# How many column pairs have their first two products made before the second tokens are normalised: nine and nine in place of five and six

## The chip, the cores and the metric

The kernel is one layer of a diffusion backbone on one core of a Trainium2 chip. A core has TensorE (PE) for matrix products, with weight loads (PEld) beside the products, VectorE (DVE), ScalarE (ACT), GpSimd (POOL) and SyncE (SP), from which this kernel issues its transfers between DRAM and the on-chip memory. Each engine works through its own list of instructions in order and waits on semaphores for the others. Products land in PSUM, from where ACT or DVE fetch them.

The metric is the device time of one execution in microseconds (us), as a median of several runs.

## The reference

1024 latent tokens and 256 context tokens of width 1024 in float32. Each layer is a half step of a gated feed-forward network, then the mixers (a short convolution and attention, merged by gates), then a second half step. Ahead of each stands a normalisation with shift and scale:

```python
x = x + 0.5 * ml[2] * swiglu(modulate(rms_norm(x, norm1_g), ml[0], ml[1]), ffn1_w_in, ffn1_w_out)
hx = modulate(rms_norm(x, norm2_g), ml[3], ml[4])
bg_l, cg_l, vc_l, q_l, k_l, v_l, gt_l = jnp.split(hx @ w_in, SPLITS, axis=-1)
...
x = x + ml[5] * merge_branches(y_conv_l, o_l, gt_l, w_branch_conv, w_branch_attn, w_out)
x = x + 0.5 * ml[8] * swiglu(modulate(rms_norm(x, norm3_g), ml[6], ml[7]), ffn2_w_in, ffn2_w_out)
return rms_norm(x, final_g)
```

What matters here are two of its products: `hx @ w_in` in the mixers, of which 20 pairs of blocks of 128 columns are made in the way described below (queries, keys and values go another way), and the product with `ffn2_w_in` in the second half step, 22 pairs.

## The kernel before

**Three products for one.** Each float32 operand is split into a high part (a copy rounded to float32r, by ACT) and a low part (the difference, by DVE), function `split`. A product is then three matmuls: high by high, high by low, low by high.

**Pairs of columns, seven products.** The latent tokens stand transposed on the chip, in two halves: the first 512 tokens (`C0`) and the second 512 (`C1`). Class `Winograd` makes a pair of column blocks for both halves at once, by Strassen's scheme in Winograd's form: the inner dimension of 1024 is cut in two, the weights of the pair form a 2 by 2 block matrix and the tokens another, and seven block products replace eight. Each product (`product(i)`) has four inner steps of three matmuls 128 x 128 by 128 x 512, twelve in all. Its left operand is a block of weights or a sum of blocks (POOL makes the sums `s1`, `s2`, `s3` and one more; `parts` splits each), its right operand is `self.r[i]`, four split tiles made from the normalised tokens. `r[1]` and `r[2]` need the first tokens alone. `r[3]` to `r[7]` need the second tokens too.

The order within a pair is fixed: `first` makes products 1 and 2 and keeps `u` (product 1) and `c` (their sum). `second` makes 6, 7 and 4, `third` makes 5 and 3, and each adds its products to the running sums on DVE.

**Started pairs.** `norm1` normalises the second tokens: sums of squares over the partitions and a broadcast on PE, and then, for each of four steps `k`, two scalings on DVE, two shifts on ACT, four differences on DVE, and five tiles of `r` that are split (ACT and DVE). While this goes on PE has only products 1 and 2 to make. So `start` makes them for the first `n_ahead` pairs, with the steps of `norm1` in between:

```python
for i in range(self.n_ahead):
    t = wpool.tile([P, 2, 512], F32, tag="wh", name=uniq("uc"), bufs=W_BUFS)
    u, c = t[:, 0], t[:, 1]
    act.copy(out=u, in_=self.product(1))
    run(norm, 1)
    dve.tensor_add(out=c, in0=u, in1=self.product(2))
    if i < RESIDENT:
        self.started.append((u, c))
    else:
        self.put_aside(t)
run(norm)
```

`norm1` has six steps (the sums, the broadcast, and the four `k`). `uc` takes two of the four `wh` buffers for good until its pair is finished (`RESIDENT` is 2); the other started pairs share the remaining two, and `put_aside` stores each to DRAM (`ucd`, 512 KB, from SP). When a pair's turn comes, `next_first` takes it out of `started`, and `fetch` brings `u` and `c` of the pair behind it back, one pair ahead, into two of the 11 buffers `t` (two loads of 256 KB). A pair that wasn't started goes through `first` in its turn.

**Weights.** The generator `lefts` gives the split left operands in the order in which they are used. For the first `n_ahead` pairs it loads the first block alone (a `raw` buffer of 512 KB, three of them) and splits its two halves; in the turn of a pair it loads both blocks (2 x 512 KB), lets POOL form the sums, and skips the two halves that have been used. Four `wl` buffers hold split operands, so ACT and DVE work up to four products ahead.

**Order.** The program is written in one order, and a planner in the compiler of the kernel places the instructions on the engines by its own costs: of what is ready, what was written earlier goes first; buffers of a pool are given out in the same way. What the planner put down is fixed in the program, and each engine follows it.

**Where it stands.** In the mixers `mix` (line 1027) takes its number from `AH2`; `mix.start(norm1)` (line 1071) begins when the first half step's output product is done, and its turns follow in the loop at 1088, with the context tokens' normalisation `normc2` (two steps after a pair) and the convolution's DVE instructions in between. In the second half step `fast` (line 1461) takes its number from `AH3`; its `start` is called in `ffn` (line 759) behind the output projection of the mixers, and its turns follow, two pairs at a time with their part of the output product. The first half step has a start of its own (`start_together`, `AH1`).

Of the kernel before, what the change touches and what calls it, by code (L numbers as in the profile page):

```python
# [41 lines left out]
STEPS = (0, 6, 6, 6, 7, 7, 8, 8, 8, 15)  # L42
WAIT = 4
AH1, WH = 8, (4, 5, 6, 7, 10, 11, 14, 15)
RESIDENT, AH2, AH3 = 2, 5, 6
SLOT = 1024


# [1526 lines left out]
```

## Time and profile before

| | us |
|---|---|
| median of 3 runs | 2805.99 (2802.83 to 2806.69) |
| the profiled execution | 2801.0 |
| its span, from the first instruction to the last | 2799.2 |
| PE busy | 2716.4 |
| DVE busy | 1956.4 |
| ACT busy | 1105.1 |
| POOL busy | 502.6 |

The mean granted clock of TensorE was 0.987 of full speed. The profile's instruction groups bear the line of a helper (88) throughout, so they are told apart by their tiles: `ps<-r,wl` are the matmuls of `Winograd`, `wl<-raw` and `wl<-s` the splits of weights and of sums of weights, `r<-nt` and `r<-h` the splits of right operands, `uc<-uc,ps` the sum that ends a started pair. Matmuls overlap, so the busy time of one is longer than the time until the next begins. A time in square brackets is how long an engine stood idle before an instruction, with the instruction whose end it waited for.

### The profile page before, as it was taken

The page shows a single profiled execution, that of the slowest core. Times are in us where ns is not written, and L with a number is a line of the kernel's source. Part 1 is how long each engine was busy: PE and PEld are TensorE (multiplying, and loading weights), DVE is VectorE, ACT ScalarE, POOL GpSimd, SP SyncE. Part 2 cuts the span into 40 slices and gives each one's busy share as a digit, 9 for nine tenths or more (in the row PEclk, how much of TensorE's full clock was granted, in tenths as well). Part 3 has the DMA queues.
Part 4 walks back from the last instruction along what each step waited for, and adds up shares of the span by engine and source line. Part 5 has one row for each costly group of instructions (what it writes and reads, how often), then busy time and mean ns, then how long its engine had stood idle before and what let it go on. Part 6 is the DMA issues. An engine that isn't in the chain of part 4 may idle for free.

```text
span 2799.2 us, 36980 instructions
## 1 busy us (share of the span) xinstructions
PE 2716.4 (97%) x13741; PEld 2280.3 (81%) x13741; DVE 1956.4 (70%) x3269; ACT 1105.1 (39%) x2177; POOL 502.6 (18%) x383
## 2 busy tenths in 40 slices
PE   7898999999999989999999999999998999999998
PEld 4687988888888867888999888877886788888887
DVE  5887688877854398676478676675458766666667
ACT  4524333333433243333244665674235222332225
POOL 2240122121000043323023111000002221212110
PEclk8899999999999999999999999999999999999999
DMA  8264434445974333322312321002433311111111
GB/s 305 95 204 156 143 107 128 131 145 162 314 237 126 103 123 106 98 90 77 119 33 84 95 80 46 27 31 80 158 91 103 101 46 46 61 61 53 46 53 68
DMA packets 355229, 302.96 MB, mean 108 GB/s; under 512 B 25558, under 2 KB 284776, under 8 KB 355048
## 3 DMA queue, kind: packets, MB, share of 16 engines
q1 hardware_dynamic: 355048, 300.59, 33.3%
q8 instruction: 108, 1.77, 0.3%
q14 instruction: 73, 0.60, 0.1%
HBM read 251.73 MB, written 48.76 MB: 107 GB/s over the span
## 4 chain that ended last, share of the span: by engine, by line
PE 54%; DVE 4%; ACT 1%; issue 1%; DMA 1%; DVEq 0%; ACTq 0%
PE ps L88 48%; PE po L88 3%; PE pt L88 3%; DVE wl L88 1%; DVE xb L88 0%; DMA raw<-in_ffn_w_out_dram 0%; DVE r L88 0%; DVE u L88 0%; DVE nt L88 0%; DVE ol L88 0%; DVE wo L88 0%; ACT pts L88 0%; DVE pts L88 0%; ACT pl L88 0%; DVE uc L88 0%
## 5 line engine op out<-in xcount | busy, mean ns | idle before, releaser
L88 PE MATMUL ps<-r,wl 128*128 128x512 f32 x5280 | 1237.7, 393 | 31.8 <-ACT wl L88 9.6
L88 PEld LDWEIGHTS ps<-r,wl 128*128 128x128 f32 x5280 | 992.2, 189 | 250.2 <-ACT wl L88 11.9
L88 POOL TENSOR_TENSOR s<-raw 128x512 f32<-128x512 f32 x64 | 100.7, 1573 | 1100.0 <-DVE r L88 377.5
L88 ACT CAST wl<-s 128x512 fp32r<-128x512 f32 x256 | 158.3, 620 | 318.9 <-PE ps L88 266.3
L88 ACT CAST wl<-raw 128x512 fp32r<-128x512 f32 x230 | 142.5, 621 | 251.9 <-PE ps L88 170.6
L88 DVE TENSOR_TENSOR wl<-raw,wl 128x512 fp32r<-128x512 f32 x228 | 163.0, 715 | 96.9 <-ACT wl L88 95.9
L88 POOL TENSOR_TENSOR s<-raw,s 128x512 f32<-128x512 f32 x64 | 102.5, 1601 | 686.1 <-DVE wl L88 682.5
L88 DVE TENSOR_TENSOR wl<-s,wl 128x512 fp32r<-128x512 f32 x256 | 215.8, 844 | 9.7 <-ACT wl L88 7.7
L88 PE MATMUL ps<-hid,wh 128*128 128x512 f32 x704 | 217.2, 390 | 0.7 <-ACT wh L88 0.7
L88 DVE SCALAR_TENSOR_TENSOR x<-ps,gate_l,x 128x512 f32<-128x512 f32 (+1 forms) x200 | 140.7, 726 | 76.7 <-PE ps L88 76.5
L88 ACT CAST wh<-raw 128x1024 fp32r<-128x1024 f32 (+2 forms) x92 | 89.4, 976 | 198.0 <-PE ps L88 167.8
L88 PEld LDWEIGHTS ps<-hid,wh 128*128 128x128 f32 x704 | 131.7, 188 | 29.5 <-ACT wh L88 1.6
L88 DVE SCALAR_TENSOR_TENSOR macc<-rawm,silu_c,macc 128x512 f32<-128x512 f32 x168 | 140.8, 856 | 15.2 <-DMA rawm<-in_w_mod_dram 14.1
L88 PE MATMUL ps<-hid,wo 128*128 128x512 f32 (+1 forms) x552 | 147.8, 381 | 2.3 <-DVE x L88 2.3
L88 DVE TENSOR_TENSOR u<-u,ps 128x512 f32<-128x512 f32 x168 | 114.2, 680 | 45.4 <-PE ps L88 45.0
L88 DVE TENSOR_TENSOR wl<-raw,wh 128x1024 fp32r<-128x1024 f32 (+1 forms) x84 | 98.4, 1172 | 65.5 <-ACT wh L88 64.0
L88 PE MATMUL ps<-wh,r 128*128 128x256 f32 x768 | 141.6, 285 | 0.0
L88 DVE TENSOR_TENSOR pts<-pt,pts 128x512 fp32r<-128x512 f32 x160 | 108.6, 686 | 43.1 <-ACT pts L88 41.9
L88 PE MATMUL ps<-hid,wl 128*128 128x512 f32 x352 | 136.5, 389 | 0.0
L88 PE MATMUL ps<-gh,wo 128*128 128x512 f32 (+1 forms) x368 | 135.0, 380 | 0.0
L88 DVE TENSOR_REDUCE m<-ps 128x1 f32<-128x512 f32 (+1 forms) x192 | 110.9, 595 | 26.6 <-PE ps L88 25.6
L88 ACT CAST pts<-pt 128x512 fp32r<-128x512 f32 x160 | 93.1, 593 | 86.2 <-PE pt L88 84.6
(254 smaller groups left out, 4784.4 us busy)
## 6 DMA issues: line engine op xcount, KB each, us to landing
raw<-in_ffn_w_in_dram SPq DMA_DIRECT2D x114, 512.0 KB, 3.7
raw<-in_ffn_w_out_dram SPq DMA_DIRECT2D x76, 512.0 KB, 4.3
rawm<-in_w_mod_dram SPq DMA_DIRECT2D x128, 256.0 KB, 3.9
raw<-in_w_in_dram SPq DMA_DIRECT2D x57, 512.0 KB, 3.6
hid<-hd SPq DMA_DIRECT2D x44, 256.0 KB, 6.1
rawm<-in_w_mod_dram SPq DMA_DIRECT2D x16, 512.0 KB, 7.3
xd<-x SPq DMA_DIRECT2D x32, 256.0 KB, 2.5
x<-xd SPq DMA_DIRECT2D x32, 256.0 KB, 5.9
```

The source lines that it names most:

```text
L88: inst = getattr(self.engine, name)(*args, **kw)
```

## The change

One line of constants. `RESIDENT` stays at 2.

```diff
-RESIDENT, AH2, AH3 = 2, 5, 6
+RESIDENT, AH2, AH3 = 2, 9, 9
```

Nine pairs of the 20 in the mixers, and nine of the 22 in the second half step, have their first two products made in `start`; seven of each nine are stored to DRAM and fetched in their turn, where it were three and four. The six steps of `norm1` are written between the first six of them in both places; in the mixers the sixth stood behind the fifth pair. The pairs 6 and up (counted from 0) are written behind all of `norm1`, and with the last of them the loads and POOL sums for the first pair's turn. The products, and what is computed, stay the same.

## The prediction

> **What bounds the kernel now.** I read the page first: busy times, then the 40 slices, then the stages by windows.
>
> ```profile
> PE 2716.4 (97%) x13741; PEld 2280.3 (81%) x13741; DVE 1956.4 (70%) x3269; ACT 1105.1 (39%) x2177; POOL 502.6 (18%) x383
> PEclk8899999999999999999999999999999999999999
> PE 54%; DVE 4%; ACT 1%; issue 1%; DMA 1%; DVEq 0%; ACTq 0%
> ```
>
> TensorE sets the time: 97% busy, and the chain that ended last is mostly PE. The change adds and removes no matmul, so all it can win is time in which PE stood still or ran at a low clock, in the two stages that it touches. The windows view, in slices of 10 us (busy us and instruction count of PE, PEld, DVE, ACT, POOL, then granted clock, DMA share, GB/s), shows them. The first row is the yardstick.
>
> ```profile
> 1100.00:1200.00 100.00, 100.00 (x443) 82.82 (x442) 68.47 (x106) 32.09 (x55) 30.52 (x22) 1.00 0.29 90
> 990.00:1000.00 10.00, 6.16 (x21) 4.62 (x20) 10.00 (x18) 6.78 (x12) 0.73 (x1) 0.84 0.26 105
> 1000.00:1010.00 10.00, 7.54 (x27) 4.54 (x26) 9.32 (x16) 5.26 (x10) 8.49 (x2) 0.98 0.64 210
> 1010.00:1020.00 10.00, 8.16 (x25) 6.04 (x25) 8.45 (x10) 5.75 (x13) 3.30 (x2) 0.66 0.01 2
> 1020.00:1030.00 10.00, 9.07 (x40) 6.98 (x39) 9.13 (x18) 2.62 (x5) 3.34 (x2) 1.00 0.47 144
> 2130.00:2140.00 10.00, 5.03 (x23) 3.83 (x21) 10.00 (x15) 5.22 (x9) 4.54 (x3) 1.00 0.44 158
> 2140.00:2150.00 10.00, 9.25 (x27) 6.58 (x28) 9.96 (x14) 4.26 (x8) 3.70 (x3) 0.66 0.36 106
> 2150.00:2160.00 10.00, 7.71 (x30) 5.08 (x29) 9.15 (x11) 4.98 (x9) 4.31 (x3) 1.00 0.15 52
> 2160.00:2170.00 10.00, 8.87 (x39) 6.78 (x38) 8.56 (x13) 3.66 (x6) 2.44 (x2) 1.00 0.32 99
> ```
>
> 443 matmuls in 100 us are one per 0.2257 us, or 44.3 in a slice. I count matmuls, not busy time, because a matmul at half clock counts as busy twice as long. Mixers (the stage that starts near 963): 21 + 27 + 25 + 40 = 113 where 177.2 fit, so 64.2 are missing, **14.5 us**. Second half step (it starts near 2100): 23 + 27 + 30 + 39 = 119, 58.2 are missing, **13.1 us**. In the same slices DVE is at 8.5 to 10 of 10. The timeline of PE says what ended the stalls (idle time in brackets):
>
> ```profile
> 977.84 15.01 PE L88 MATMUL ps<-r,wl 128*128 128x512 f32 x65
> 996.70 8.15 PE L88 MATMUL ps<-r,wl 128*128 128x512 f32 x26 [3.84 <-ACT wl L88]
> 1005.26 1.51 PE L88 MATMUL ps<-r,wl 128*128 128x512 f32 x5 [0.42 <-DVE r L88]
> ...
> 1013.94 7.35 PE L88 MATMUL ps<-r,wl 128*128 128x512 f32 x24 [1.30 <-DVE r L88]
> ...
> 2117.53 17.50 PE L88 MATMUL ps<-r,wl 128*128 128x512 f32 x76
> 2140.01 0.94 PE L88 MATMUL ps<-r,wl 128*128 128x512 f32 x2 [4.98 <-ACT wl L88]
> ```
>
> PE finishes its started pairs at 992.85 and 2135.03. It then waits for the first split weight of product 6, and after that piece by piece for `r`, the operands that `norm1` makes on DVE. The timeline of DVE shows that `norm1` is late because DVE does it one instruction every 0.60 us:
>
> ```profile
> 978.13 1.28 DVE L88 TENSOR_TENSOR h<-x,pt 128x512 f32<-128x512 f32 x2 [0.68 <-PE pt L88]
> ...
> 984.80 0.67 DVE L88 TENSOR_TENSOR uc<-uc,ps 128x512 f32<-128x512 f32 x1
> 985.40 0.68 DVE L88 TENSOR_TENSOR r<-h,r 128x512 fp32r<-128x512 f32 x1
> 986.00 0.68 DVE L88 TENSOR_TENSOR wl<-raw,wl 128x512 fp32r<-128x512 f32 x1
> ...
> 1012.13 2.96 DVE L88 TENSOR_TENSOR r<-nt,r 128x512 fp32r<-128x512 f32 x3
> ...
> 1016.51 0.69 DVE L88 TENSOR_TENSOR r<-nt,r 128x512 fp32r<-128x512 f32 x1
> ...
> 2117.81 1.29 DVE L88 TENSOR_TENSOR h<-x,pt 128x512 f32<-128x512 f32 x2 [0.42 <-PE pt L88]
> ...
> 2154.86 1.88 DVE L88 TENSOR_TENSOR r<-nt,r 128x512 fp32r<-128x512 f32 x3
> ...
> 2158.59 0.69 DVE L88 TENSOR_TENSOR r<-nt,r 128x512 fp32r<-128x512 f32 x1
> ```
>
> So `norm1` runs from 978.1 to 1017.2 and from 2117.8 to 2159.3, and PE's cover ends 24 us before its end in both.
>
> **The change, part by part.**
>
> *More cover.* A started pair is two products of 12 matmuls: 24 x 0.2257 = 5.42 us of PE. Mixers get 4 more (21.7 us), the second half step 3 more (16.3 us). The cover now ends at 992.85 + 21.7 = 1014.5 and 2135.03 + 16.3 = 2151.3. Product 6 asks for its last operand r6[3] after 9 more matmuls, 2.0 us later: 1016.5 and 2153.3. It was there at 1015.1 and 2156.7 (ends of the rows with x3).
>
> *What the cover costs DVE.* Each started pair brings forward three DVE instructions (two weight splits, one sum of products), 1.8 us. Nothing is added in total, since the same three drop out of the pair's later turn. `norm1` from its first row on is 44 instructions: 4 steps of 2 scalings, 4 subtractions, 5 low parts. In mixers 10 others ran among them (counted between its first row and its last); now it is the 10 splits and 7 sums of the pairs that are then still to come, 17. (44 + 17) x 0.60 = 36.6 us, with 2 us for gaps in its chain an end at 1016.7; before, gaps and slow instructions were 39.1 - 54 x 0.60 = 6.7 us, with which it ends at 1021.4. r6[3] comes some 2.1 us before the end, at 1014.6 to 1019.3, against 1016.5 when PE asks: a stall of 0 to 2.8 us. In the second half step 13 others become 16: (44 + 16) x 0.60 + 2 gives 2155.8, with the old 41.5 - 57 x 0.60 = 7.3 us of gaps 2161.1; r6[3] 2.6 us earlier, 2153.2 to 2158.5, against 2153.3: 0 to 5.2 us. I take 2.0 us in mixers. In the second half step I take 4.0, near the upper end, for its weights come late as well:
>
> ```profile
> 2135.39 2.26 POOL L88 TENSOR_TENSOR s<-raw 128x512 f32<-128x512 f32 x1 [347.07 <-DVE r L88]
> ```
>
> POOL's first sum of weight columns waited for DVE, by my reading for one of the 11 `t` buffers that `norm1` holds, and PE got its weight 4.6 us after that sum began. The sum is now emitted behind all of `norm1`, which frees DVE of POOL's company but leaves the weight just in time.
>
> *Half clock.* In slices of 2 us:
>
> ```profile
> 998.00:1000.00 2.00, 2.00 (x6) 1.61 (x5) 2.00 (x4) 0.20 (x1) 0.73 (x1) 0.50 0.17 68
> 1012.00:1014.00 2.00, 0.70 (x3) 0.07 (x1) 2.00 (x3) 0.00 (x0) 1.33 (x1) 0.50 0.00 0
> ```
>
> After the stalls PE ran at clock 0.50; the counting above holds that loss already. The Trainium skill (TensorE: Matmul & The Clock Gate, Part 1) says that the clock halves only after about 3.4 us without work and comes back after as much work. By that my 4.0 us stall would cost an estimated 1.7 us more, and the sum below would be 17.9. The second row speaks for a looser rule: no gap between 1004.7 and 1013.9 was over 1.3 us. I leave it out of the sum and keep it in the range.
>
> *Saved and fetched pairs.* All but two started pairs go to DRAM and come back: 4 and 3 more stores on SP (512 KB), twice as many loads (256 KB), and 4 and 3 more loads of a half weight block (512 KB).
>
> ```profile
> 2126.91 0.59 ACT L88 COPY uc<-ps 128x512 f32<-128x512 f32 x1 [0.84 <-PE ps L88]
> ...
> 2119.77 0.34 SPq L88 DMA_DIRECT2D ucd<-uc  x1
> ...
> DMA to landing us min/median/max: 2.5/2.9/5.6
> ```
>
> A store waits on SP for the pair's DVE sum, and the weight loads of later pairs are queued behind it; ACT's copy two pairs on waits for the store to land, with operand casts behind it. The store issued at 2119.77 landed by about 2123, 4 us before the copy at 2126.91; even 5.6 us would be in time. I cost it at 0; if that cover goes, the price is rival B's.
>
> *Denser turns.* A started pair's later turn is five products, 60 x 0.2257 = 13.5 us instead of 19.0, with the same POOL work and loads. Mixers now have nine such turns, not five.
>
> ```profile
> 1050.00:1060.00 10.00, 9.07 (x41) 7.17 (x40) 10.00 (x20) 1.82 (x4) 4.40 (x4) 1.00 0.50 159
> 1070.00:1080.00 10.00, 9.25 (x41) 7.35 (x40) 10.00 (x13) 2.23 (x5) 4.94 (x3) 1.00 0.37 127
> 2300.00:2400.00 100.00, 100.00 (x443) 82.81 (x442) 67.09 (x95) 32.54 (x55) 17.67 (x13) 1.00 0.19 58
> ```
>
> The first two rows fall into such turns: 0.93 and 0.75 us of PE idle over some 3.7 turns, 0.5 us each. Four more: 2.0 us (0 if DVE's backlog was the cause, since it shrinks). The second half step has none in its started turns (third row): 0 for three more.
>
> *Sum.* Mixers 14.5 - 2.0 - 2.0 = 10.5. Second half step 13.1 - 4.0 = 9.1. Together 19.6 us. The profiled execution took 2801.0 us (span 2799.2 and 1.8 around it): it would take 2781.4. The runs shown have a median of 2805.99, 5.0 above it; the forecast for a median is 2805.99 - 19.6 = **2786.4 us**.
>
> **The rivals.**
>
> *A: `norm1` is pushed back by all that is brought forward* (DVE in order, sums and splits ahead of it). r6[3] then comes 4 x 1.8 = 7.2 us later at 1022.3 and 3 x 1.8 = 5.4 later at 2162.1: stalls of 5.8 and 8.8 us, each with some 5 us at half clock as before, 2.5 us. Back come 5.8 + 2.5 + 2.0 + 8.8 + 2.5 = 21.6 of 27.6; 6.0 are left: 2800.0. For it: DVE is full throughout. Against it: POOL's sums leave the stretch, and the last pairs' sums can come after.
>
> *B: slower, by the SP queue in the denser turns.* A turn needs two weight loads; on SP they stand behind fetches of saved products that wait for a `t` buffer.
>
> ```profile
> 1057.26 1.30 POOL L88 TENSOR_TENSOR s<-raw 128x512 f32<-128x512 f32 x1 [3.75 <-DMA raw<-in_w_in_dram]
> ...
> 1070.39 1.61 POOL L88 TENSOR_TENSOR s<-raw 128x512 f32<-128x512 f32 x1 [3.82 <-DMA raw<-in_w_in_dram]
> ```
>
> POOL waited 3.8 us a turn for such a load. If PE paid that in each of 7 further turns, 26.6 us: 2805.99 - 19.6 + 26.6 = 2813.0. It decides from 19.6 / 7 = 2.8 us a turn. Against it: today's price to PE is 0.5.
>
> *C: the seam keeps its gap.* The late weight of product 6 (the 3.84 and 4.98 us) is a matter of the order on ACT and POOL, and stands, with its 2.5 us of half clock, wherever the started pairs end: 27.6 - 6.3 - 7.5 - 2.0 leaves 11.8, 2794.2. The longer cover then does only half of what it says. For it: both stages show such a gap at just that place. Against it: with `norm1` nearly done, ACT and POOL have little else to do.
>
> **How the numbers follow.** Forecast, with its bounds (stalls 0 to 2.8 and 0 to 5.2, turns 0 to 4): 0.62, from 2778.4 (all 27.6 won) to 2790.4. C 0.12. A 0.18, some of it won by more than 0.2%. B 0.08. A measurement of this kernel can tell about 0.2%, 5.6 us, from no change. Faster: 0.62 + 0.12 + 0.05 of A = 0.79. Slower: 0.07 of B. Same: the rest, 0.14. The range has to hold the forecast, C and the nearer half of A: 2778 to 2800.
>
> **What would show it.** Right: PE in mixers without a gap to about 1014 and in the second half step to 2151, one gap under 5 us behind it, the slices of 10 us with 40 matmuls or more, clock 1.00; last `r` on DVE at 1017 to 1022 and 2156 to 2161. A: those ends at 1024 and 2165, long waits for `r`. B: PE waits for `wl` every 13.5 us between 1030 and 1140, POOL waits for `raw`. C: one gap near 4 us for ACT `wl`. It would also be wrong if the stages outside these two moved.

## The result, and the profile after

| | before | after |
|---|---|---|
| median of 5 runs each, us | 2805.99 (2801.89 to 2807.14) | 2776.89 (2776.47 to 2781.59) |
| the profiled execution, us | 2801.0 | 2781.05 |
| its span, us | 2799.2 | 2779.2 |

The ratio of the times is 0.9908, with a 95% interval of 0.9897 to 0.9919: 25.8 us less of 2805.99 (22.7 to 28.9), which puts the time at 2780.2. The forecast was 2786.4, 19.6 us less, in a range of 2778 to 2800. So the change is faster, by somewhat more than the forecast. By the ratio, which takes in all five runs of each kernel, the time lies inside the range; the median of after's five runs, 2776.89, lies 1.1 us below its lower end. The first part of the page of after:

```profile
PE 2712.2 (98%) x13741; PEld 2280.0 (82%) x13741; DVE 1960.7 (71%) x3269; ACT 1103.4 (40%) x2177; POOL 497.0 (18%) x383
```

The instructions are as many as before on every engine, and the chain that ended last has the same shares, 54% of it PE. PE is still the bound; it has 20.0 us less of span around the same matmuls. The windows of after, in the slices in which the prediction counted (columns as there):

```profile
990.00:1000.00 10.00, 10.00 (x46) 8.29 (x45) 9.81 (x18) 6.77 (x13) 0.00 (x0) 1.00 0.61 189
1000.00:1010.00 10.00, 10.00 (x45) 8.27 (x45) 9.38 (x16) 6.74 (x13) 0.68 (x1) 1.00 0.62 195
1010.00:1020.00 10.00, 9.77 (x43) 7.78 (x42) 9.91 (x12) 3.86 (x8) 5.09 (x4) 1.00 0.44 157
1020.00:1030.00 10.00, 9.23 (x37) 6.29 (x37) 10.00 (x11) 3.66 (x8) 5.21 (x4) 1.00 0.57 188
1050.00:1060.00 10.00, 10.00 (x46) 8.29 (x45) 10.00 (x16) 2.32 (x5) 5.24 (x3) 1.00 0.66 210
1060.00:1070.00 10.00, 9.71 (x44) 7.41 (x43) 9.76 (x22) 2.34 (x4) 2.44 (x2) 1.00 0.32 92
2130.00:2140.00 10.00, 10.00 (x46) 8.29 (x45) 9.29 (x13) 4.63 (x9) 5.22 (x3) 1.00 0.64 211
2140.00:2150.00 10.00, 10.00 (x45) 8.11 (x44) 10.00 (x13) 4.67 (x9) 4.49 (x3) 1.00 0.54 168
2150.00:2160.00 10.00, 7.92 (x25) 5.48 (x25) 9.11 (x13) 4.20 (x8) 2.76 (x3) 0.83 0.11 42
2160.00:2170.00 10.00, 10.00 (x46) 8.28 (x45) 8.29 (x12) 3.82 (x7) 5.57 (x4) 1.00 0.34 107
```

Counted in the same way: in the mixers 46 + 45 + 43 + 37 = 171 matmuls where 177.2 fit, 1.4 us lost (before, 14.5). In the second half step 46 + 45 + 25 + 46 = 162, 3.4 us lost (before, 13.1), nearly all in one slice, with the clock at 0.83. PE's timeline shows where the rest went; a number in brackets is idle time:

```profile
981.58 37.22 PE L88 MATMUL ps<-r,wl 128*128 128x512 f32 x163
1019.03 1.89 PE L88 MATMUL ps<-r,wl 128*128 128x512 f32 x7 [0.23 <-DVE wl L88]
1021.17 2.29 PE L88 MATMUL ps<-r,wl 128*128 128x512 f32 x7 [0.25 <-ACT r L88]
1023.96 22.89 PE L88 MATMUL ps<-r,wl 128*128 128x512 f32 x99 [0.50 <-DVE r L88]
...
2106.95 43.70 PE L88 MATMUL ps<-r,wl 128*128 128x512 f32 x191
2150.90 0.73 PE L88 MATMUL ps<-r,wl 128*128 128x512 f32 x2 [0.25 <-DVE r L88]
2153.24 0.50 PE L88 MATMUL ps<-r,wl 128*128 128x512 f32 x1 [1.60 <-ACT r L88]
2153.96 18.67 PE L88 MATMUL ps<-r,wl 128*128 128x512 f32 x74 [0.22 <-DVE r L88]
```

Stalls of 0.98 us are left in the mixers and of 2.07 us in the second half step. The long waits for `wl` are gone.

**Stages.** Slices of 10 us shift with the program, so I also measured each stage from its first matmul `ps<-r,wl`, in every profile: from the start of the mixers to the start of the second half step, and from there to the end of the span.

| kernel | mixers start | mixers, us | second half step, us | span |
|---|---|---|---|---|
| before | 963.19 | 1136.72 | 699.29 | 2799.2 |
| after | 966.92 | 1122.42 | 689.86 | 2779.2 |

The mixers won 14.3 us and the second half step 9.4, 23.7 together. The first half step ended 3.7 us later in after's profile, though the two programs have the same instructions in the same order on every engine up to the mixers. Most of it arose in one place. PE's timeline there, in before and then in after:

```profile
594.85 5.73 PE L88 MATMUL ps<-r,wl 128*128 128x512 f32 x24 [2.56 <-ACT u L88]
600.42 0.40 PE L88 MATMUL pt<-acch,ones_r 128*1 128x512 f32 x1
```

```profile
595.91 8.35 PE L88 MATMUL ps<-r,wl 128*128 128x512 f32 x24 [3.20 <-ACT u L88]
604.11 0.40 PE L88 MATMUL pt<-acch,ones_r 128*1 128x512 f32 x1
```

Both kernels wait there for ACT's copy `u`. In after the wait was 0.64 us longer, and the 24 matmuls behind it ran for the most part at half clock (the granted clock from 596 to 600 us was 0.50, in before 1.00) and took 8.35 us, not 5.73. The row behind them starts 3.69 us later: 2.63 us by the clock, 0.64 by the wait, and 0.42 that had arisen ahead of it. From there to the start of the mixers both take 362.8 us (963.19 - 600.42 and 966.92 - 604.11). So the profiled pair's 20.0 us, which comes so close to the summed 19.6, is 23.7 less a loss in a stage that the change doesn't touch; that it comes so close is luck. The five runs of each kernel lie in two groups 4 to 5 us apart (2801.9 and 2802.8 against 2806.0 to 2807.1; 2776.5 to 2776.9 against 2781.1 and 2781.6), as this place could make them. That link is not shown: those executions have no trace, and the 15 runs of before that were timed beside e5 to e8 show no two groups, but spread evenly from 2800.9 to 2807.5.

### The profile page after: what moved, and what is told of

Same layout as the page of the kernel before. It is cut to its first block, busy times and chain, and to the rows that moved or that the text cites. A ratio compares the mean times of both kernels' runs of the same rounds, so it can differ in the third digit from the quotient of the medians.

```text
span 2779.2 us, 37038 instructions
## 1 busy us (share of the span) xinstructions
PE 2712.2 (98%) x13741; PEld 2280.0 (82%) x13741; DVE 1960.7 (71%) x3269; ACT 1103.4 (40%) x2177; POOL 497.0 (18%) x383
## 4 chain that ended last, share of the span: by engine, by line
PE 54%; DVE 4%; ACT 1%; issue 1%; DMA 1%; DVEq 0%; ACTq 0%
PE ps L88 48%; PE po L88 3%; PE pt L88 3%; DMA raw<-in_ffn_w_out_dram 1%; DVE wl L88 1%; DVE u L88 1%; DVE wo L88 0%; DVE r L88 0%; DVE ol L88 0%; DVE pts L88 0%; ACT pts L88 0%; DVE v L88 0%; DVE uc L88 0%; DVE m L88 0%; ACT yf L88 0%
## 5 line engine op out<-in xcount | busy, mean ns | idle before, releaser
L88 DVE SCALAR_TENSOR_TENSOR macc<-rawm,silu_c,macc 128x512 f32<-128x512 f32 x168 | 141.6, 860 | 13.1 <-DMA rawm<-in_w_mod_dram 11.7
L88 DVE TENSOR_REDUCE m<-ps 128x1 f32<-128x512 f32 (+1 forms) x192 | 111.1, 596 | 28.9 <-PE ps L88 28.0
```

Source lines behind the costliest of these rows:

```text
L88: inst = getattr(self.engine, name)(*args, **kw)
```

## The experiments

**Theory:** before, PE stood at the seam because its cover ended before DVE's chain through `norm1`; longer cover wins that time, in each stage by itself. **Rivals:** the order on ACT and POOL keeps the gap (C in the prediction); denser turns and their transfers take part of the win back (B); or the win comes from a program that was laid out anew as a whole, not from the two seams. All kernels below were timed against before, in several rounds; "us less" is taken from the ratio and the median of before in the same rounds; the stages are from their profiles, as above.

| kernel | pairs | ratio, interval | us less | mixers start | mixers | second |
|---|---|---|---|---|---|---|
| e1_mixers_only | 9, 6 | 0.9948 (0.9936 to 0.9961) | 14.6 | 965.87 | 1122.97 | 699.26 |
| e2_second_only | 5, 9 | 0.9954 (0.9941 to 0.9968) | 12.9 | 969.16 | 1137.42 | 689.02 |
| e3_seven | 7, 7 | 0.9958 (0.9945 to 0.997) | 11.8 | 965.31 | 1131.66 | 694.63 |
| e4_twelve | 12, 12 | 0.988 (0.9867 to 0.9894) | 33.7 | 967.02 | 1119.32 | 684.06 |
| e5_less_dve | 5, 6 | 0.9978 (0.9969 to 0.9987) | 6.2 | 964.00 | 1134.34 | 695.86 |
| e6_seven_less_dve | 7, 7 | 0.9925 (0.9912 to 0.9937) | 21.0 | 968.28 | 1125.69 | 689.93 |
| e7_double_store | 12, 12 | 0.9879 (0.9865 to 0.9892) | 33.9 | 964.30 | 1118.06 | 684.24 |
| e8_macc_dve | 12, 12 | 0.988 (0.9865 to 0.9895) | 33.7 | 967.84 | 1118.29 | 683.47 |

Where two kernels have the same number of pairs in a stage and differ only elsewhere, that stage agrees to 0.8 us (1136.72 and 1137.42; 1122.42 and 1122.97; 699.29 and 699.26; 689.86 and 689.02); the three kernels with twelve pairs agree to 1.3 us. The time ahead of the mixers varies from 963.2 to 969.2 whatever the kernel, so single stages tell more than the whole.

**One stage alone.**

```diff
-RESIDENT, AH2, AH3 = 2, 5, 6
+RESIDENT, AH2, AH3 = 2, 9, 6
```

> Nine started pairs in the mixers alone, six as before in the second half step. Theory 1 (cover: PE stood still for want of work until norm1 was done on DVE, each stage for itself): the mixers' share alone, 14.3 us by the two profiles, so about 2806.0 - 14.3 = 2791.7, ratio 0.995; the second half step keeps its 4.98 us gap. Rival (the planner lays out the whole program anew, and the gain is spread over stages that the change doesn't touch): no fixed share, the two single changes do not add up to the 25.8 us of both.

```diff
-RESIDENT, AH2, AH3 = 2, 5, 6
+RESIDENT, AH2, AH3 = 2, 5, 9
```

> Nine started pairs in the second half step alone, five as before in the mixers. Theory 1: the second half step's share alone, 9.4 us by the two profiles, about 2796.6, ratio 0.9966; the mixers keep their 3.84 us gap and their 2 us slices at clock 0.50. Rival (new layout of the whole program): not the rest of 25.8 us.

Each moved its own stage by what that stage moved in after (mixers 13.8 and 14.3, second half step 10.3 and 9.4) and left the other where it was. The timed wins add up: 14.6 + 12.9 = 27.5 against 25.8, inside its interval. The rival of a program laid out anew falls.

**How the win grows with the pairs.**

```diff
-RESIDENT, AH2, AH3 = 2, 5, 6
+RESIDENT, AH2, AH3 = 2, 7, 7
```

> Seven started pairs in both stages. Theory 1 (each further pair is 5.4 us of cover until norm1 is done): two pairs more in the mixers, 10.8 of the 14.3 us, one more in the second half step, 5.4 of the 9.4 us: 16.2 us off, 2789.8, and a gap at both seams that is shorter than before. Rival (late weight: the gap stood there because POOL's first sums were written before norm1's last step and had to share its buffers; from the seventh pair on they stand behind it): with seven the gap is gone already, 22 to 25 us off, 2781 to 2784.

11.8 us less (8.4 to 15.4): under both expectations. Mixers won only 5.1 for two pairs, and then 9.2 for two more; the second half step won 4.7 for one pair. PE's timeline of this kernel, then ACT's and POOL's, show why:

```profile
979.96 25.89 PE L88 MATMUL ps<-r,wl 128*128 128x512 f32 x113
1016.32 24.14 PE L88 MATMUL ps<-r,wl 128*128 128x512 f32 x95 [10.47 <-ACT wl L88]
```

```profile
1000.14 1.62 POOL L88 TENSOR_TENSOR s<-s,raw 128x512 f32<-128x512 f32 x1
```

```profile
1013.05 0.62 ACT L88 CAST r<-nt 128x512 fp32r<-128x512 f32 x1 [4.19 <-DVE nt L88]
...
1014.09 1.65 ACT L88 CAST r<-nt 128x512 fp32r<-128x512 f32 x3
1015.65 1.13 ACT L88 CAST wl<-s 128x512 fp32r<-128x512 f32 x2
```

The weight sum that product 6 needs was done by POOL at 1001.76. Its cast stands on ACT behind the casts of `norm1`'s last step, and ACT waited 4.19 us for that step's `nt`, with the cast of the finished sum behind. PE stood 10.47 us, all for one weight. This is rival C, not at nine pairs but at seven: where the planner puts the first turn's weight casts among `norm1`'s on ACT decides when the seam opens. (In the second half step PE stood 5.24 us for ACT's `wl`.) Compare after: its first cast stands ahead of that step.

```profile
1012.55 0.62 ACT L88 CAST wl<-s 128x512 fp32r<-128x512 f32 x1 [1.24 <-POOL s L88]
...
1018.41 0.62 ACT L88 CAST r<-nt 128x512 fp32r<-128x512 f32 x1 [2.11 <-DVE nt L88]
```

```diff
-RESIDENT, AH2, AH3 = 2, 5, 6
+RESIDENT, AH2, AH3 = 2, 12, 12
```

> Twelve started pairs in both stages: 65 us of cover, past the end of norm1 in both. Theory 1: what is left at the seam of the second half step (4.4 us by matmul count) goes too and nothing else changes, 2772 to 2774. Rival (each stored pair costs PE time in its denser turn, 0.5 us): 6 more such turns, 3 us back, 2775 to 2780. If the SP queue with its ten stores in a row starves the weight loads, slower than with nine: over 2780.

33.7 us less, the best version: 0.988 (0.9867 to 0.9894). That is 7.9 us more than nine pairs, where the expectation had 4.4 left to win; the part on the base of 13.1 us below says why. PE's timeline shows no wait at all at the seams. In the mixers, the timeline of DVE shows `norm1`'s end, that of POOL its first sum:

```profile
981.67 74.17 PE L88 MATMUL ps<-r,wl 128*128 128x512 f32 x326
...
2103.96 77.34 PE L88 MATMUL ps<-r,wl 128*128 128x512 f32 x340
```

```profile
1024.52 0.69 DVE L88 TENSOR_TENSOR r<-nt,r 128x512 fp32r<-128x512 f32 x1
```

```profile
1026.75 1.29 POOL L88 TENSOR_TENSOR s<-raw 128x512 f32<-128x512 f32 x1 [334.47 <-DMA raw<-in_w_in_dram]
```

Twelve denser turns in each stage, and 20 stores in place of before's 7, cost nothing that shows. Rival B falls.

**Less work for DVE in `norm1`**, on before and then on seven pairs. The low parts of `r[5]` and `r[7]` aren't made, and PE reads the high parts in their place: 8 DVE instructions fewer.

```diff
-            split(src, t[:, 0], t[:, 1], lo_eng)
+            if i in self.bare:
+                act.copy(out=t[:, 0], in_=src)
+            else:
+                split(src, t[:, 0], t[:, 1], lo_eng)
...
-            matmul(ps, wh, r[:, 1], start=False, stop=False)
+            matmul(ps, wh, r[:, 0 if i in self.bare else 1], start=False, stop=False)
...
+    mix.bare = 5, 7
...
+    fast.bare = 5, 7
```

> The kernel before (five and six started pairs), with the low parts of the right operands of products 5 and 7 left out in the mixers and the second half step: their high parts are read in their place, so PE has the same matmuls and ACT the same casts, and DVE eight instructions fewer in each norm1, 8 x 0.60 = 4.8 us. Theory 1 (PE waits for norm1, and norm1 goes at DVE's pace): each stage gains 3 to 5 us, together 6 to 10, 2796 to 2799. Rival (the seam is held by the first turn's weights, whatever DVE does in norm1): the gaps of 3.84 and 4.98 us stay and the gain is under 3 us.

> Seven started pairs in both stages, with the same eight DVE instructions left out of each norm1. With seven pairs PE stood 10.47 us at the seam of the mixers for the first turn's weight, though POOL's sum for it was ready some 14 us earlier: on ACT its cast is queued behind the casts of norm1's last step, which wait for DVE. If that is so (the seam opens when DVE reaches norm1's last step), the gap shortens by the six instructions left out of the first three steps, 3.6 us, in both stages, to some 6.9 and 1.6, and the run is 7 to 9 us under that of seven pairs, 2784 to 2786. Rival (the weight is late for POOL or its load): the gap stays at 10 us, 2792 to 2794.

On before: 6.2 us less (3.6 to 8.7 by the interval), at the low end of the theory's 6 to 10; the second half step won 3.4, the mixers 2.4, under the 3 to 5 expected of a stage. PE's timeline of e5:

```profile
996.21 8.99 PE L88 MATMUL ps<-r,wl 128*128 128x512 f32 x31 [2.55 <-ACT wl L88]
1008.65 1.22 PE L88 MATMUL ps<-r,wl 128*128 128x512 f32 x2 [3.46 <-DVE r L88]
```

The first gap shrank from 3.84 us to 2.55, but a wait for `r` of 3.46 us followed, where before's were 0.42 to 1.30: PE still ran ahead of DVE. On seven pairs the same edit won more, 10.3 us against e3 by the medians (2793.36 and 2783.11; 10.7 by the stages). PE's and ACT's timelines of e6:

```profile
982.94 25.89 PE L88 MATMUL ps<-r,wl 128*128 128x512 f32 x113
1009.74 0.73 PE L88 MATMUL ps<-r,wl 128*128 128x512 f32 x2 [0.91 <-ACT wl L88]
1013.02 17.20 PE L88 MATMUL ps<-r,wl 128*128 128x512 f32 x62 [2.55 <-DVE wl L88]
```

```profile
1009.07 0.61 ACT L88 CAST wl<-s 128x512 fp32r<-128x512 f32 x1
1012.40 0.62 ACT L88 CAST r<-nt 128x512 fp32r<-128x512 f32 x1 [2.72 <-DVE nt L88]
```

Expected was a gap of some 6.9 us; PE waited 0.91 us for the weight's high part and 2.55 for its low part. Here the weight's cast stands ahead of `norm1`'s last step. Counted from the start of the run of 113 matmuls that both kernels have, the cast came after 26.1 us (1009.07 - 982.94) and not 35.7 (1015.65 - 979.96), and the last step's first cast after 29.5 and not 33.1. So 3.6 us of the shift are the shorter `norm1`, and 6.0 are the place of the cast. The edit did two things at once, and its 10.3 us cannot be given to DVE alone.

**What the stores cost**, on twelve pairs: each pair put aside is stored twice.

```diff
             sp.dma_start(out=ucd[:], in_=t[:])
+            spare = dram.tile([P, 2, 512], F32, name=uniq("ucd2"))
+            sp.dma_start(out=spare[:], in_=t[:])
```

> Twelve started pairs, each of the ten that are put aside in both stages stored a second time to a place that nobody reads: 20 more stores of 512 KB on SP, each behind the pair's DVE sum and ahead of the weight loads. My prediction costed the stores at 0: within 2 us of twelve pairs, 2770 to 2774. Rival (SP's queue is near its limit while pairs are started, and a buffer comes free later): PE waits for weights in both starts, 5 us or more.

33.9 us less than before, where e4 has 33.7: 24 more stores of 512 KB (10 in each of the two stages, 4 in the first half step) cost nothing that can be measured. The mixers took 1118.06 us against 1119.32.

**The place in the first half step**, on twelve pairs: the high part of the modulation's sums is made on DVE, not on ACT, so that ACT's copy `u` no longer stands behind it.

```diff
-                split(acc, ah, al)
+                split(acc, ah, al, None, dve)
```

> Twelve started pairs, and in later_mod the high part of the sums for shift, scale and gate is copied by DVE, not ACT. In the first half step's turns ACT's copy of product 1 is queued behind that cast, which waits for a DVE chain; PE stands 2.6 to 3.5 us there, and the matmuls behind the gap ran at half clock in some profiles and not in others. If that gap is what sets the profile's 20.0 us apart from the 25.8 of the timed runs, it is gone here: 4 to 6 us under twelve pairs, 2766 to 2768, with a smaller spread. Rival: DVE is full there (87 of 100 us), and the copies lengthen its chain by as much: 2770 to 2774.

No gain: 33.7 us as e4. The wait moved and shrank, in PE's timeline of e8:

```profile
600.75 3.06 PE L88 MATMUL ps<-r,wl 128*128 128x512 f32 x12 [1.10 <-DVE c L88]
```

But the mixers began at 967.84, not earlier than in e4 (967.02); where the time went instead isn't shown. In e4's profile this place was at full clock already, so there was little to win, and the spread of the times didn't shrink (2768.5 to 2773.0; in e4, 2769.9 to 2772.2). What costs 3.7 us in after's profile is therefore shown by its rows, but wasn't taken away by a run.

## Why the prediction was right

*More cover: right.* It put the end of PE's cover 51.3 us (1014.5) and 51.4 us (2151.3) after the start of the stage. PE's first gap came after 51.9 us (1018.80 - 966.92) in the mixers, where the cover ended. In the second half step it came after 61.3 us (2150.65 - 2089.34), 10 us beyond it, for a reason that stands below.

*The end of `norm1`: too early, in both stages.* The last `r` was to come at 1016.7 to 1021.4 and 2155.8 to 2161.1, 53.5 to 58.2 and 55.9 to 61.2 us after the start of the stage. DVE's timeline of after:

```profile
1022.62 1.28 DVE L88 TENSOR_TENSOR r<-nt,r 128x512 fp32r<-128x512 f32 x2
...
1024.43 1.78 DVE L88 TENSOR_TENSOR wl<-raw,wl 128x512 fp32r<-128x512 f32 x1
1026.13 1.77 DVE L88 TENSOR_TENSOR wl<-s,wl 128x512 fp32r<-128x512 f32 x1
1027.83 1.77 DVE L88 TENSOR_TENSOR nt<-nt,x 128x512 f32<-128x512 f32 x1
...
1030.72 0.68 DVE L88 TENSOR_TENSOR r<-nt,r 128x512 fp32r<-128x512 f32 x1
...
2153.21 0.69 DVE L88 TENSOR_TENSOR r<-nt,r 128x512 fp32r<-128x512 f32 x1 [0.68 <-ACT r L88]
```

It ended 64.5 us (1031.40 - 966.92) and 64.6 us (2153.90 - 2089.34) after the start: later than rival A has it in the mixers (1024), and 6.3 and 3.4 us beyond the late end of the forecast. Two steps failed. One is the count of other DVE instructions among the 44 of `norm1`: the timeline has 23 in the mixers and 21 in the second half step, not 17 and 16, for splits of the first turn's weights were placed among them too. At 0.60 us each that is 3.6 and 3.0 us. The other is "the sum is now emitted behind all of `norm1`, which frees DVE of POOL's company". The planner put POOL's sums into `norm1` all the same, in the mixers from 1009.32 on (the row stands in the last section), and beside each of seven a DVE instruction took up to 1.8 us, where alone it takes 0.68: some 7.2 us in all. With twelve pairs the first sum of the mixers did stand behind (1026.75), no DVE instruction of `norm1` was slowed, and it ended after 58.2 us (1025.21 - 967.02), with the same 23 others among its own.

Why did it cost so little? The order of PE's instructions in after's program tells (row, tiles, count). In the mixers, from the first turn on, where `ps_9106` is product 6, `r_1528` its last operand r6[3], `ps_9151` product 4 and `r_1529` r4[3]:

```
2655 L88 MATMUL ps_9106<-r_1479_8746,wl_9036 128x512 x3
2656 L88 MATMUL ps_9106<-r_1496_8813,wl_9036 128x512 x3
2657 L88 MATMUL ps_9106<-r_1513_8880,wl_9036 128x512 x3
2658 L88 MATMUL ps_9106<-r_1528_8941,wl_9036 128x512
2659 L88 MATMUL ps_9124<-r_1477_8740,wl_9056 128x512 x2
2660 L88 MATMUL ps_9151<-r_1480_8750,wl_9073 128x512 x2
2661 L88 MATMUL ps_9168<-r_1478_8743,wl_9103 128x512 x2
2662 L88 MATMUL ps_9106<-r_1528_8941,wl_9036 128x512 x2
...
2675 L88 MATMUL ps_9151<-r_1529_8945,wl_9073 128x512
```

*The boundary stall of 2.0 us in the mixers: too large, 0.98.* Product 6 does ask for r6[3] after nine matmuls, as the prediction has it. But the planner put six matmuls of three other products between the use of its high part and of its low part, and PE waited 0.25 us for the high part (1021.17) and 0.50 us for the low (1023.96); the other 0.23 us were for the low part of product 6's weight. r6[3] was whole some 57 us after the start (1023.9), 0.9 us past the late end of the predicted 51.4 to 56.1 (1014.6 to 1019.3). The very last `r` belongs to a product that asks for it only 46 matmuls after product 6 begins. So rival A was right that `norm1` ends late, and it still cost PE only these 0.75 us. The weaving was nothing that the prediction counted on: here it had luck.

*The boundary of 4.0 us in the second half step: near in size by the four slices, for other reasons.* There the planner wove the first four products together, and product 6 asks for r6[3] after 35 matmuls, not 9; "asks for its last operand r6[3] after 9 more matmuls" failed in this stage. PE got past the end of its cover by 43 matmuls, 9.7 us, before it first waited, 0.25 us for r6[3]. The 1.60 and 0.22 us behind it were for r4[3], the very last `r`, which came 3.4 to 8.7 us later than the prediction has it. So the stall was of the predicted size for an operand that the prediction didn't name. By the count in the four slices 3.4 us were lost: 2.07 are gaps, and half clock behind them accounts for the rest, as the windows in slices of 2 us suggest:

```profile
2152.00:2154.00 2.00, 0.54 (x2) 0.23 (x2) 1.32 (x3) 1.44 (x3) 0.00 (x0) 1.00 0.04 13
2154.00:2156.00 2.00, 2.00 (x6) 1.62 (x7) 1.86 (x4) 0.22 (x1) 0.00 (x0) 0.63 0.00 0
```

No gap there was over 1.60 us, and yet the clock fell to 0.63. The Trainium skill (TensorE: Matmul & The Clock Gate, Part 1) names an idle window of some 3.4 us as the condition. By these rows gaps of 0.25, 1.60 and 0.22 us within 3.3 us are enough, as the prediction's row at 1012 suggested.

*The 13.1 us of the second half step: too small a base.* The four slices don't hold all that PE loses there. Windows over the first 100 us of the stage, in before, after and e4:

```profile
2099.91:2199.91 100.00, 88.96 (x377) 69.54 (x376) 83.59 (x128) 44.34 (x76) 24.18 (x15) 0.97 0.31 100
2089.34:2189.34 100.00, 96.49 (x423) 78.36 (x422) 85.11 (x132) 49.27 (x85) 23.20 (x15) 0.98 0.41 132
2086.34:2186.34 100.00, 100.00 (x452) 83.07 (x451) 83.34 (x129) 52.83 (x91) 18.46 (x12) 1.00 0.47 151
```

Against twelve pairs before misses 75 matmuls, 16.9 us at 0.2257 us each, and nine pairs still miss 29, 6.5 us (by the stages, 15.2 and 5.8). Part of it stands behind the slices, as a wait of 1.44 us for ACT's `wo` at 2180. So the base of 13.1 and the 4.0 left at the boundary were both too small, and the two errors cancel: that the stage won 9.4 us for the predicted 9.1 is in part luck. In the mixers, windows of that kind hold 380, 441 and 454 matmuls, 16.7 us to win, against the prediction's 14.5 and the 1.7 of the two waits that it booked under denser turns; 2.9 are left. Nor was "all 27.6 won" a bound: twelve pairs won 33.7 us.

*Denser turns at 2.0 us in the mixers: the term that was mis-sized most there.* The old waits in the slices from 1050 and 1070 are gone, and one of 0.24 us is left between 1030 and 1085 (the slice from 1060, with 9.71). Of the bounds, 0 was the right end. That DVE's backlog was the cause is not shown: PE waited there for DVE's `wl`, but DVE is at 10.00 in the slice from 1050 before and after. The mixers' 14.3 us, for the predicted 10.5, follow from this and from the smaller stall: 14.5 less the 1.4 that the count still misses, and the old waits of 0.93 and 0.75 us less the 0.24, which is 14.5. This is most of the 4.1 us by which the stages' 23.7 exceed the forecast's 19.6; the 2.1 us from there to the timed 25.8 lie within its interval.

*Stores and fetches at 0: right* (e4, e7). *Rival B: false*; nothing like its 2.8 us a turn arose with 24 denser turns (e4). *Rival C: false at nine pairs, true at seven*, where it cost 10.47 us and not the 3.84 it was priced at. *Half clock left out of the sum:* it did occur in the second half step, and makes up to 1.4 us there by the four slices (3.4 less 2.07), which the range had room for.

## What to carry to other kernels

Cover for a chain on another engine should outlast the chain: at nine pairs PE and `norm1` still met, at twelve they didn't, and the two stages won 8.9 us more. The worth of a unit of cover is not its length: from five pairs to seven, nine and twelve the mixers won 5.1, 9.2 and 3.1 us, since a ready weight stuck in order behind a late operand on ACT can keep the seam shut. Count lost matmuls, not idle time, over a stretch that reaches past the last slow slice, and compare stage by stage from a mark in the program; a whole-span difference that fits the forecast may be two errors that cancel.

## What the runs showed of the hardware

**DVE waits out a POOL instruction.** POOL's timeline in after, beside the DVE rows above:

```profile
1009.32 1.50 POOL L88 TENSOR_TENSOR s<-raw 128x512 f32<-128x512 f32 x1 [315.62 <-DMA raw<-in_w_in_dram]
...
1024.12 1.54 POOL L88 TENSOR_TENSOR s<-raw 128x512 f32<-128x512 f32 x1 [3.76 <-DMA raw<-in_w_in_dram]
1025.74 1.62 POOL L88 TENSOR_TENSOR s<-s,raw 128x512 f32<-128x512 f32 x1
1027.32 1.73 POOL L88 TENSOR_TENSOR s<-raw,raw 128x512 f32<-128x512 f32 x1
```

The last three POOL instructions end at 1025.66, 1027.36 and 1029.05; the three DVE instructions that began within them end at 1026.21, 1027.90 and 1029.60, each 0.54 or 0.55 us later, a little less than one instruction's own 0.68. POOL took 1.29 us for the same work where it began behind `norm1` (e4). The Trainium skill (SBUF — State Buffer, Who interferes with whom) says that a DVE instruction with two inputs from the on-chip memory and a POOL instruction that reads it take turns, the second waiting until the first ends. The trace agrees, at 1.1 us for each such pair here.

**The same stall may or may not halve the clock.** In the first half step, gaps of 2.56 us (before), 2.64 (e5), 2.69 (e4) and 2.89 (e3) left the 24 matmuls behind them at 5.73 or 5.74 us; 2.16 us (e7), 2.78 (e6), 2.93 (e2), 3.20 (after) and 3.46 (e1) left 7.38, 8.54, 8.47, 8.35 and 8.28. The shortest gap slowed them and four longer ones didn't, so the length of the gap alone doesn't decide. It makes some 2.7 us of difference between executions that run the same code up to that point.
